# A two-layer hybrid block: the adaptive-norm background is placed elsewhere and fetched further ahead, and operand splits and weight sums of the feed-forward layers go from GpSimd to VectorE

## The chip, the cores and the metric

The kernel runs on one core of a Trainium2 chip, in one launch. The metric is the device time of an execution in microseconds (us). The core has five engines with a queue each, and a queue is worked off in order: TensorE (PE in the rows; its weight loads stand as PEld), VectorE (DVE), ScalarE (ACT), GpSimd (POOL) and SyncE (SP), which here only issues transfers.

## The reference

The input is x of 1024 tokens by 1024 features. There are two layers of two sub-blocks each. Every sub-block is wrapped in the same way:

```python
shift, scale, gate = split(silu(c) @ ada_w[layer, s] + ada_b[layer, s], 3)
h = rms_norm(x, norm_pre[layer, s]) * (1.0 + scale) + shift
y = sub_block(h)
x = x + gate * rms_norm(y, norm_post[layer, s])
```

Sub-block 0 of layer 0 is a mixer of two recurrent groups (gated delta rule and RWKV-7), sub-block 0 of layer 1 is a gated linear recurrence (RG-LRU), and sub-block 1 of both layers is a feed-forward layer of width 2816: `(silu(h @ w_gate) * (h @ w_up)) @ w_down`. All data is float32.

## The kernel before

The order of the program is: start and mixer, then three sub-blocks in `layers` (L893): n = 0, the feed-forward layer 0; n = 1, the recurrence; n = 2, the feed-forward layer 1. Tokens are worked in two halves of 512 columns, h = 0 and h = 1.

**Products.** A float32 operand is split into a high part (ScalarE casts it to fp32r) and a low part (the operand minus the high part, a subtraction of two tiles). A product of 512 features takes 12 matmuls: high by high, high by low and low by high, for 4 tiles of 128 rows. One pass of 512 columns is one matmul.

**Feed-forward** (`ffn`, L656). Gate and up projection of both halves are computed with seven products in place of eight, on sums and differences of the token operands (`operands`, L711) and of the weights (`sums`, L739). It has 22 steps f of 128 output columns. `first(f)` (L695) does two of the seven products, which need no sums; `second(f)` and `third(f)` do the other five. The first 10 or 14 `first` are run ahead of `operands`, the last four of them between its four parts. `rest` (L792) then runs second and third of every f, and in its later part the `first` that are still left. So a step is 5 products in the first twelve or so steps and 7 after.

**Who does what before.** `operands` makes five operands for each of four k: up to 6 additions on VectorE, five casts on ScalarE (L734) and five low parts (L735). Of the low parts, GpSimd takes those for which `out in (t3, b22)` holds: Python compares the lists by value, so for k = 0, where the lists are empty, that is four of five, and two of five for k = 1 to 3: ten in a layer. In every step `sums` has two additions on GpSimd (L744 and L746) and two on VectorE (L745, L747), and `third` lets GpSimd make the low part of one weight operand (`parts(a22, nc.gpsimd)`, L770). `first` makes two low parts on GpSimd.  VectorE also reads the results out of PSUM (L759, L761, L764, L774, L778) and multiplies them.

**Down projection** (`down`, L591). 22 (or 8) weight rows k for each of two column halves, in four PSUM banks. In the middle of the first column half it calls `aside`, which can start the next sub-block's norm.

**The background.** `ada_steps` (L500) computes one sub-block's shift, scale and gate on VectorE: six blocks of 512 columns (0 to 3 are shift and scale, 4 and 5 the gate), each of eight additions (L478, L480) of a 128x512 weight tile that a 256 KB transfer brings (L515). A block's sum is held in a tile of the ring `ad` (4 buffers), the weight tiles in three fixed tiles that are free after the mixer (`abufs`: g2, w2a2, k16; shown as g, w2a, k). A block ends with a small matmul into the one PSUM bank `es`, which `second` also uses. `operands` uses the ring `ad` too. A call of `tick` (L240) advances the background by one addition. Ticks stand in `down` (one for each k), in `rest` (one for each f) and in the recurrence's projections; `park` finishes a block, `drain` everything.

**What sets the order.** The code is written as one program; the framework's planner puts each engine's instructions in order before the run: at each point an instruction whose inputs and buffers are there may go, the earliest in the program first. So an addition of the background may be issued well before its place in the program. Once planned, an engine's queue is fixed, and an instruction that waits holds up all behind it on that engine. All transfers go through SyncE's queue.

Of the kernel before, what the change touches and what calls it, by code (L numbers as in the profile page):

```python
# [15 lines left out]
ALU = mybir.AluOpType  # L16
# [56 lines left out]
class Block:  # L73
# [426 lines left out]
    def ada_steps(self, l, s, tag, blocks, res, gtag):  # L500


        nc, a = self.nc, self.a
        w = a["ada_w"][l, s]
        if 0 in blocks:
            ab = self.c.tile([128, 24], F32, name=f"ab{l}{s}")
        res["G"] = []
        for cb in blocks:
            acc = self.t(tag, [128, 512])
            self.held = True  # L510
            for k in range(KD):
                st = next(self.abufs, None)
                if st is None:
                    st = self.t(tag, [128, 512])
                nc.sync.dma_start(st, w[k * 128:(k + 1) * 128, cb * 512:(cb + 1) * 512])  # L515
                self.ada_add(acc, st, k)
                yield
            if cb < 4:
                self.ada_put(ab, self.ada_total(acc), cb, l, s)
                if cb == 3:  # L520
                    res["A"], res["B"] = ab[:, 16:24], ab[:, 0:8]
            else:
                ps = self.t("es", [128, 512])
                o = (cb - 4) * 512
                br = self.t(tag, [128, 512])
                nc.sync.dma_start(br[0:1], a["ada_b"][l, s:s + 1, 2048 + o:2560 + o])
                nc.vector.tensor_tensor(acc[0:1], acc[0:1], br[0:1], ALU.add)
                self.mm(ps, self.ones, acc)
                wp = self.t(tag, [128, 512])
                nc.sync.dma_start(wp, a["norm_post"][l, s, o:o + 512].partition_broadcast(128))  # L530
                g = self.t(gtag, [128, 512])
                nc.vector.tensor_tensor(g, ps, wp, ALU.mult)
                res["G"].append(g)
            self.held = False
            yield
# [120 lines left out]
    def ffn(self, l, hs):  # L656
# [54 lines left out]
        def operands(xs):  # L711

            tags = iter(("p",) * 12 + ("s1",) * 8 + ("cy",) * 12 + ("s2",) * 4)
            A = E
            for k in range(4):
                v12 = self.modulated(self.turned_x(xs, k, ("sb", "es")), *self.AB, k, "ad")
                v22 = self.modulated(self.turned_x(xs, k + 4, ("sa",)), *self.AB, k + 4, "ad")
                (h1, l1), (h2, l2) = b11[k], b21[k]
                d1 = A()
                tt(d1, v12, f32(h1), ALU.subtract)  # L720
                tt(d1, d1, f32(l1), ALU.subtract)
                d2 = A()
                tt(d2, v22, d1, ALU.subtract)
                tt(v12, v22, v12, ALU.subtract)
                for full, out in ((d2, t2), (d1, t1), (v12, t3), (v22, b22), (None, t4)):
                    if full is None:
                        tt(d2, f32(h2), d2, ALU.subtract)
                        tt(d2, d2, f32(l2), ALU.add)
                        full = d2
                    if out is t4 and k > 1:  # L730
                        hi, lo = self.pair("ar")
                    else:
                        hi, lo = self.t(next(tags), [128, 512], F32R), self.t(next(tags), [128, 512], F32R)
                    nc.scalar.copy(hi, full)  # L734
                    (nc.gpsimd if out in (t3, b22) else nc.vector).tensor_tensor(lo, full, hi, ALU.subtract)  # L735
                    out.append((hi, lo))
                yield

        def sums(f):  # L739

            a11, a12 = fetch("ffn_w_gate", f)
            a21, a22 = fetch("ffn_w_up", f)
            s1, s2, s3, s4 = Y(), E(), E(), Y()
            nc.gpsimd.tensor_tensor(s1, a21, a22, ALU.add)  # L744
            tt(s2, s1, a11, ALU.subtract)  # L745
            nc.gpsimd.tensor_tensor(s3, a11, a21, ALU.subtract)  # L746
            tt(s4, a12, s2, ALU.subtract)  # L747
            return s1, s2, s3, s4, a22

# [17 lines left out]
        def third(f):  # L767

            s0, s4, a22, u2, u3, pc, pd = kept.pop(f)
            w3, w4 = parts(s4), parts(a22, nc.gpsimd)  # L770
            product(pd, w3, b22, False)
            following(f + 1)
            y = E()
            tt(y, pd, u2, ALU.add)  # L774
            self.act(y, y, AF.Silu)
            product(pc, w4, t4, False)
            tt(u3, u3, y, ALU.mult)
            tt(u2, pc, u2, ALU.add)  # L778
            tt(u2, u2, s0(), ALU.mult)  # L779
            for h, g in ((1, u3), (0, u2)):  # L780
                hi = self.t("yx", [128, 512], F32R)
                nc.scalar.copy(hi, g)  # L782
                tt(g, g, f32(hi), ALU.subtract)
                nc.sync.dma_start(self.gpart(h, f, 0), f32(hi))
                nc.sync.dma_start(self.gpart(h, f, 1), g)
# [3 lines left out]
                w = sums(f)  # L789
                kept[f, "w"] = w + (parts(w[1]),)  # L790

        def rest(ahead):  # L792
            following(0)
            for f in range(NF):
                second(f)
                if ahead <= f + 1 < NF:
                    first(f + 1)
                third(f)
                self.tick()

        return first, operands, rest

# [90 lines left out]
    def layers(self, hs, AB, x1, x2, x3, late):  # L893
# [3 lines left out]
        res = [dict() for _ in subs]  # L897
        for n, (l, x_in, x_out) in enumerate(subs):
            if n == 0:
                self.bg = chain(self.ada_steps(0, 1, "ad", (4, 5), res[0], "st"), self.ada_steps(1, 0, "ad", range(6), res[1], "gb"))  # L900
            else:
                self.bg = self.ada_steps(*ids[n + 1], "ad", range(6), res[n + 1], "st") if n + 1 < len(subs) else iter(())
            self.AB = AB
            gs = {}
            if l is not None:
                first, operands, rest = self.ffn(l, hs)
                if n == 0:
                    for f in range(PRE):
                        first(f, True)
                    xs = late()  # L910
                    self.deepen()
                ahead = (PRE if n == 0 else 0) + MID
                for f in range(ahead - MID, ahead - 4):
                    first(f, True)
                self.park()
                for f, _ in zip(range(ahead - 4, ahead), operands(xs)):
                    first(f, True)
                rest(ahead)
            for h in range(2):
                keep = h == 1 and l is None  # L920
                if l is None:
                    self.pool_lo = True
                    ys, w = self.lru(h, hs)
                    self.pool_lo = False
                    lhs = lambda k, half: ys[k]
                else:
                    w = self.a["ffn_w_down"][l]
                    for f in range(AHEAD if h == 0 else 0):
                        gs[0, f] = self.load_g(0, f)

                    def lhs(k, half):
                        if half == 0 and h == 0 and k + AHEAD < NF:
                            gs[0, k + AHEAD] = self.load_g(0, k + AHEAD)
                        g = gs[h, k]
                        if half == 1 and h == 0 and k >= 2:
                            gs[1, k - 2] = self.load_g(1, k - 2)
                        return g

                    if h == 1:
                        for f in (NF - 2, NF - 1):  # L940
                            gs[1, f] = self.load_g(1, f)
                nxt = []

                def aside():
                    if h == 0:
                        if l is None:
                            nxt.append(self.prenorm(x_in, 1, *AB))
                    elif n + 1 < len(subs):
                        self.drain()
                        nxt.append((res[n + 1]["A"], res[n + 1]["B"]))  # L950
                        nxt.append(self.prenorm(x_out, 0, *nxt[0]))

                last = n + 1 == len(subs) and h == 1
                xs = self.down(lhs, w, h, x_in, x_out, res[n]["G"], F_BANKS[4:] + F_BANKS[:4],
                               "s2" if keep else "yx", ("cy", 6) if keep else ("ht", 7) if last else (None, 0), keep, aside,
                               "lru" if l is None else None)
                if nxt:
                    hs = nxt[-1]
                    if h:
                        AB = nxt[0]  # L960
# [607 lines left out]
```

## Time and profile before

Times of three runs: 2782.76, 2784.68 and 2784.86 us; the median is 2784.68. The profiled execution took 2782.86 us, its span (first to last instruction) 2781.1 us.

| engine | busy us | share of the span |
|---|---|---|
| TensorE | 2639.1 | 95% |
| VectorE | 1779.6 | 64% |
| ScalarE | 1176.4 | 42% |
| GpSimd | 553.3 | 20% |

Shares are means over stages that differ. The stretches that the change touches are, in us from the span's start: operands of layer 0 from 1062 to 1109, its steps to about 1480, its down projection to 1720, the recurrence to about 2080, operands of layer 1 from 2116 to 2163, its steps to about 2525. "Granted clock" is the share of full speed that TensorE was given: 1.0 is 2.4 GHz, 0.5 is 1.2 GHz.

### The profile page before, as it was taken

Reading aid. Unit: us, or ns where it says so; the run is one execution under the profiler, and the core shown is the slowest. Engines: PE = TensorE matmul, PEld = TensorE weight load, DVE = VectorE, ACT = ScalarE, POOL = GpSimd, SP = SyncE. Lnnn points to the kernel's source line nnn. Section 1 sums busy time; section 2 is a strip of 40 time slices with the busy share of each in tenths; the row PEclk is TensorE's granted clock in tenths of the full one; section 3 lists DMA queues with packets and bytes.
Section 4 is the critical chain, followed back from the end, with each engine's and each line's share of the span. In section 5 each row is a group of like instructions: output and inputs, shape, how many; then the busy total and the mean of one; then the engine's idle time right before and its main releaser. Section 6 shows DMA issues by size and latency. Waiting matters only on the chain. (4 is left out here: it accounts for less than half of the span.)

```text
span 2781.1 us, 44135 instructions
## 1 busy us (share of the span) xinstructions
PE 2639.1 (95%) x16104; PEld 2041.2 (73%) x16104; DVE 1779.6 (64%) x3224; ACT 1176.4 (42%) x2164; POOL 553.3 (20%) x440
## 2 busy tenths in 40 slices
PE   7899999999999997899999999999998899999998
PEld 3666667676766676787888778777876788888887
DVE  5677878667677556988544463996855884553233
ACT  3555564553455435233332233572645333332222
POOL 2322220002100115233330000210015333330000
PEclk9999999999999999999999999999999999999999
DMA  6644443335732374766448873888754554448753
GB/s 237 226 150 136 139 151 101 118 108 202 250 110 81 99 243 148 237 209 196 150 137 300 291 247 130 293 296 298 257 196 148 166 191 139 137 142 288 239 180 108
DMA packets 423327, 519.60 MB, mean 187 GB/s; under 512 B 32667, under 2 KB 217790, under 8 KB 423110
## 3 DMA queue, kind: packets, MB, share of 16 engines
q1 hardware_dynamic: 423110, 516.78, 56.0%
q8 instruction: 127, 2.08, 0.3%
q14 instruction: 90, 0.74, 0.1%
HBM read 367.76 MB, written 148.90 MB: 186 GB/s over the span
## 5 line engine op out<-in xcount | busy, mean ns | idle before, releaser
L98 PE MATMUL mm<-ht,wh 128*128 128x512 f32 x1920 | 658.6, 417 | 27.4 <-ACT e L701 19.1
L98 PEld LDWEIGHTS mm<-ht,wh 128*128 128x128 f32 x1920 | 352.9, 192 | 117.1 <-ACT e L701 30.0
L98 PE MATMUL mm<-ht,wl 128*128 128x512 f32 x960 | 391.4, 409 | 9.6 <-DMA wl<-pd 4.4
L675 POOL TENSOR_TENSOR wl<-wd,wh 128x512 fp32r<-128x512 f32 x99 | 130.9, 1323 | 524.0 <-ACT wh L674 483.8
L98 PEld LDWEIGHTS mm<-ht,wl 128*128 128x128 f32 x960 | 183.8, 191 | 55.1 <-DMA wl<-pd 6.0
L144 ACT CAST wh<-wd 128x512 fp32r<-128x512 f32 x168 | 104.0, 620 | 263.1 <-PE sb L98 215.3
L145 DVE TENSOR_TENSOR wl<-wd,wh 128x512 fp32r<-128x512 f32 x156 | 108.1, 694 | 161.1 <-ACT wh L144 158.8
L145 POOL TENSOR_TENSOR wl<-wf,wh 128x512 fp32r<-128x512 f32 x80 | 115.6, 1453 | 290.1 <-ACT wh L144 232.0
L552 POOL TENSOR_TENSOR sm<-sm,dv 128x1 f32<-128x1 f32 x64 | 39.4, 625 | 651.9 <-DVE sm L551 338.9
L144 ACT CAST wh<-wf 128x512 fp32r<-128x512 f32 x133 | 82.0, 619 | 157.5 <-PE sb L98 78.4
L106 ACT ACTIVATE e<-mm 128x512 f32<-128x512 f32 x120 | 71.3, 594 | 146.0 <-PE mm L98 144.0
L675 DVE TENSOR_TENSOR wl<-e,wh 128x512 fp32r<-128x512 f32 x88 | 61.3, 696 | 105.1 <-ACT wh L674 105.1
L98 PE MATMUL sa<-s,wh 128*128 128x512 f32 x392 | 121.2, 391 | 0.0
L674 ACT CAST wh<-wd 128x512 fp32r<-128x512 f32 x99 | 61.3, 621 | 131.0 <-PE sb L98 43.2
L106 ACT ACTIVATE e<-e 128x512 f32<-128x512 f32 x140 | 88.0, 631 | 57.4 <-DVE e L774 24.6
L106 ACT ACT_TABLE_LOAD x84 | 107.8, 1283 | 2.2 <-PEq L1557 0.7
L674 ACT CAST wh<-yx 128x512 fp32r<-128x512 f32 x88 | 54.6, 621 | 125.3 <-PE sb L98 48.4
L98 PEld LDWEIGHTS <-h 64*64 64x64 f16 (+1 forms) x1984 | 53.8, 106 | 73.4 <-issue 49.2
L1198 POOL TENSOR_TENSOR s<-s,k 128x512 f32<-128x512 f32 x16 | 24.7, 1543 | 340.0 <-DVE s L1441 163.5
L98 PE MATMUL sa<-wh,p 128*128 128x512 f32 x260 | 91.8, 397 | 0.0
L782 ACT CAST yx<-yx 128x512 fp32r<-128x512 f32 x88 | 54.6, 621 | 77.3 <-DVE yx L779 40.5
L98 PEld LDWEIGHTS sa<-s,wh 128*128 128x128 f32 x392 | 73.7, 188 | 15.5 <-issue 0.4
(494 smaller groups left out, 6633.5 us busy)
## 6 DMA issues: line engine op xcount, KB each, us to landing
gd<-yx SPq DMA_DIRECT2D x176, 256.0 KB
pd<-wh SPq DMA_DIRECT2D x132, 256.0 KB
pd<-wl SPq DMA_DIRECT2D x132, 256.0 KB
wd<-in_ffn_w_down_dram SPq DMA_DIRECT2D x132, 256.0 KB
wh<-pd SPq DMA_DIRECT2D x120, 256.0 KB
wl<-pd SPq DMA_DIRECT2D x120, 256.0 KB
wd<-in_ffn_w_gate_dram SPq DMA_DIRECT2D x114, 256.0 KB
wd<-in_ffn_w_up_dram SPq DMA_DIRECT2D x78, 256.0 KB
```

Of the source, the lines that this page charges most:

```text
L98: self.nc.tensor.matmul(out, lhsT=lhsT, rhs=rhs, start=start, stop=stop, skip_group_check=more)
L106: return self.nc.scalar.activation(out, in_, func, bias=bias, scale=scale)
L144: nc.scalar.copy(wh, wf)
L145: (nc.gpsimd if self.pool_lo and (self.pool_lo > 1 or k0) else nc.vector).tensor_tensor(wl, wf, wh, ALU.subtract)
L552: nc.gpsimd.tensor_tensor(r, r, self.mhalf[:, 0:1], ALU.pow)
L674: nc.scalar.copy(flat(wh), full)
L675: (eng or nc.vector).tensor_tensor(flat(wl), full, flat(wh), ALU.subtract)
L782: nc.scalar.copy(hi, g)
L1198: nc.gpsimd.tensor_tensor(im, first, one32, ALU.add)
```

## The change

Four things are changed. (1) In `operands` all low parts go to VectorE; in `sums` both GpSimd additions go to VectorE; in `third` the low part of a22 goes to VectorE. `first` stays as it is. (2) `ada_steps` issues the transfers of up to three weight tiles before the addition that uses the first of them. (3) `rest` ticks only from f = 12 on in layer 0 (from f = 0 in layer 1). (4) The background of layer 1's feed-forward layer is cut in two: its blocks 0 to 3 are appended to the background of n = 0 and go on through n = 1, and its gate blocks 4 and 5 are ticked in n = 2, where nothing was ticked before. `aside` no longer drains the background but ticks until what the next norm needs is in the program.

```diff
@@ ada_steps
-        res["G"] = []
+        res.setdefault("G", [])
...
+            sts = []
             for k in range(KD):
-                st = next(self.abufs, None)
-                if st is None:
-                    st = self.t(tag, [128, 512])
-                nc.sync.dma_start(st, w[k * 128:(k + 1) * 128, cb * 512:(cb + 1) * 512])
-                self.ada_add(acc, st, k)
+                for j in range(len(sts), min(k + 3, KD)):
+                    st = next(self.abufs, None)
+                    if st is None:
+                        st = self.t(tag, [128, 512])
+                    nc.sync.dma_start(st, w[j * 128:(j + 1) * 128, cb * 512:(cb + 1) * 512])
+                    sts.append(st)
+                self.ada_add(acc, sts[k], k)
@@ operands
-                    (nc.gpsimd if out in (t3, b22) else nc.vector).tensor_tensor(lo, full, hi, ALU.subtract)
+                    tt(lo, full, hi, ALU.subtract)
@@ sums
-            nc.gpsimd.tensor_tensor(s1, a21, a22, ALU.add)
+            tt(s1, a21, a22, ALU.add)
             tt(s2, s1, a11, ALU.subtract)
-            nc.gpsimd.tensor_tensor(s3, a11, a21, ALU.subtract)
+            tt(s3, a11, a21, ALU.subtract)
@@ third
-            w3, w4 = parts(s4), parts(a22, nc.gpsimd)
+            w3, w4 = parts(s4), parts(a22)
@@ rest
-        def rest(ahead):
+        def rest(ahead, late):
...
-                self.tick()
+                if f >= late:
+                    self.tick()
@@ layers
-                self.bg = chain(self.ada_steps(0, 1, "ad", (4, 5), res[0], "st"), self.ada_steps(1, 0, "ad", range(6), res[1], "gb"))
-            else:
-                self.bg = self.ada_steps(*ids[n + 1], "ad", range(6), res[n + 1], "st") if n + 1 < len(subs) else iter(())
+                self.bg = chain(self.ada_steps(0, 1, "ad", (4, 5), res[0], "st"), self.ada_steps(1, 0, "ad", range(6), res[1], "gb"),
+                                self.ada_steps(1, 1, "ad", range(4), res[2], None))
+            elif n == 2:
+                self.bg = self.ada_steps(1, 1, "ad", (4, 5), res[2], "st")
...
-                rest(ahead)
+                rest(ahead, 12 if n == 0 else 0)
...
-                        self.drain()
+                        while "A" not in res[n + 1] or n == 0 and len(res[1]["G"]) < 2:
+                            self.tick()
```

## Rows read from the trace of the kernel before

**Rows 1.** The page, engines: busy us (share of the span) x instructions.

```profile
PE 2639.1 (95%) x16104; PEld 2041.2 (73%) x16104; DVE 1779.6 (64%) x3224; ACT 1176.4 (42%) x2164; POOL 553.3 (20%) x440
```

**Rows 2.** Stretches: us, busy us (x instructions) by engine, granted clock, DMA share, GB/s.

```profile
1066.00:1112.00 46.00, 31.81 (x128) 24.79 (x128) 39.82 (x40) 24.60 (x44) 28.23 (x18) 0.85 0.41 130
...
1112.00:1190.00 78.00, 68.54 (x284) 54.34 (x283) 71.31 (x97) 21.53 (x36) 24.11 (x16) 0.96 0.73 237
...
1190.00:1250.00 60.00, 60.00 (x270) 49.73 (x270) 52.15 (x69) 21.61 (x36) 17.69 (x12) 1.00 0.62 205
...
1300.00:1480.00 180.00, 180.00 (x792) 147.09 (x791) 96.96 (x148) 65.54 (x111) 54.52 (x43) 1.00 0.50 161
...
2117.00:2162.00 45.00, 31.75 (x130) 24.48 (x128) 38.51 (x35) 24.25 (x43) 29.70 (x20) 0.86 0.34 111
...
2170.00:2290.00 120.00, 120.00 (x531) 99.39 (x530) 104.64 (x133) 42.63 (x71) 39.72 (x26) 1.00 0.59 193
```

**Rows 3.** TensorE's waits, 1056 to 1112: us in total, times, longest.

```profile
PE mm L98 <- ACT e L701: 6.8, 2, 3.7
PE es L98 <- ACT wh L674: 6.3, 1, 6.3
PE mm L98 <- POOL wl L675: 1.0, 1, 1.0
```

**Rows 4.** TensorE's waits, 2112 to 2170.

```profile
PE es L98 <- ACT wh L674: 7.0, 1, 7.0
PE mm L98 <- ACT e L701: 6.7, 2, 3.7
```

**Rows 5.** TensorE's waits, 1112 to 1270.

```profile
PE sb L98 <- DVE yx L761: 5.7, 3, 3.3
PE sa L98 <- DVE yx L764: 5.7, 3, 2.6
```

**Rows 6.** Stretches at half clock, columns as in rows 2.

```profile
1152.50:1159.30 6.80, 5.64 (x13) 4.46 (x14) 6.53 (x10) 1.11 (x2) 1.82 (x1) 0.50 0.76 223
1261.70:1265.10 3.40, 3.40 (x10) 2.62 (x9) 3.37 (x6) 0.63 (x1) 0.00 (x0) 0.50 0.90 278
...
2159.40:2166.20 6.80, 3.72 (x9) 2.95 (x10) 5.42 (x7) 2.28 (x4) 1.77 (x2) 0.50 0.40 116
```

**Rows 7.** VectorE in order of time: start, us, what [idle before <- releaser].

```profile
2118.38 0.68 DVE L724 TENSOR_TENSOR ad<-ad,ad 128x512 f32<-128x512 f32 x1
2118.98 0.69 DVE L723 TENSOR_TENSOR e<-ad,e 128x512 f32<-128x512 f32 x1
2125.00 1.77 DVE L727 TENSOR_TENSOR e<-ht,e 128x512 f32<-128x512 f32 x1 [5.33 <-POOL p L735]
2126.80 1.66 DVE L728 TENSOR_TENSOR e<-e,ht 128x512 f32<-128x512 f32 x1
```

**Rows 8.** GpSimd in the same stretch, in order of time.

```profile
2124.92 1.29 POOL L735 TENSOR_TENSOR p<-e,p 128x512 fp32r<-128x512 f32 x1
2126.18 1.73 POOL L735 TENSOR_TENSOR p<-ad,p 128x512 fp32r<-128x512 f32 x1
```

**Rows 9.** VectorE's waits, 1056 to 1112.

```profile
DVE cy L735 <- ACT cy L734: 0.7, 1, 0.7
```

**Rows 10.** The chain that ended last: start, us, what.

```profile
2172.68 2.72 PE sb L98 x12
```

**Rows 11.** VectorE's groups, 1112 to 1190: busy, mean ns | idle before.

```profile
L480 DVE SCALAR_TENSOR_TENSOR ad<-w2a,sc,ad 128x512 f32<-128x512 f32 x9 | 10.3, 1147 | 2.0 <-DMA w2a<-in_ada_w_dram 1.9
L480 DVE SCALAR_TENSOR_TENSOR ad<-k,sc,ad 128x512 f32<-128x512 f32 x9 | 8.8, 979 | 1.5 <-DMA k<-in_ada_w_dram 1.3
L480 DVE SCALAR_TENSOR_TENSOR ad<-g,sc,ad 128x512 f32<-128x512 f32 x8 | 7.0, 873 | 0.0
...
L761 DVE TENSOR_TENSOR yx<-sb,yx 128x512 f32<-128x512 f32 x5 | 3.4, 682 | 0.1
```

**Rows 12.** A group of GpSimd, 1112 to 1190, columns as in rows 11.

```profile
L744 POOL TENSOR_TENSOR yx<-wd,wd 128x512 f32<-128x512 f32 x6 | 9.8, 1629 | 10.6 <-DMA wd<-in_ffn_w_up_dram 8.1 <-DVE ad L480 2.5
```

**Rows 13.** TensorE's waits, 1590 to 2060.

```profile
PE sa L98 <- DVE wl L145: 8.7, 9, 1.9
PE mm L98 <- DMA wl<-pd: 4.4, 2, 3.5
```

## The prediction

> **What bounds the kernel now.** I read the page first: TensorE is busy 95% of the span [rows 1], so a gain can only come from stretches in which it stands still or runs at half clock. The table of stretches finds them. In the operands of both feed-forward layers TensorE is busy 31.8 of 46 us and 31.75 of 45 us, and in the first steps of layer 0 68.5 of 78; in the steps after that, and in those of layer 1, it is busy throughout (60.0 of 60, 120.0 of 120) [rows 2]. VectorE is the fullest other engine exactly there. The waits then name what TensorE stood for: in the operands of layer 0 14.1 us for ScalarE's casts and copies and one low part (6.8 + 6.3 + 1.0) [rows 3], in those of layer 1 13.7 us [rows 4], in the steps of layer 0 11.4 us for VectorE's reads out of PSUM (L761, L764) [rows 5]. The timeline shows why VectorE is late. Alone it starts a two-tile subtraction every 0.60 us (2118.38, 2118.98); while GpSimd works, the same operation takes 1.66 to 1.77 us (2125.00, 2126.80) [rows 7], and GpSimd's own goes from 1.29 to 1.73 [rows 8]. Reads out of PSUM stay at 0.68 in a stretch full of GpSimd work (the last of [rows 11]). So a GpSimd subtraction of two tiles takes about 1.07 us from VectorE (1.67 less 0.60), more than the 0.60 that VectorE would need to do it. Last, the chain: from 2165 to the end it is nearly all TensorE, 2.72 us per product of 12 matmuls [rows 10]; a microsecond saved ahead of it moves the end.
>
> **Operands.** Between 2117 and 2162 VectorE ran 35 instructions in 38.5 us [rows 2]. At 0.605 each that is 21.2, so 17.3 us is what GpSimd cost it. GpSimd ran 20 there: by the code ten low parts of `operands`, three weight sums, six low parts of `first`, one small one. Thirteen move. VectorE then has 48 instructions, 29.0 us; of the six low parts that stay two fall into VectorE's pause of 5.33 us and four still cost 1.07 each, 4.3. The sum is 33.3, which is 5.2 less. The pause ended with a GpSimd low part [rows 7], which waited its turn behind other GpSimd work; on VectorE it can follow its cast, and I take 1 us of the pause. New is that ten low parts wait for a cast on ScalarE, and VectorE's next additions queue behind them, and TensorE behind those through ScalarE; the one such wait shown is 0.7 us [rows 9]. I give that 0.2: 6 us gained in layer 1. In layer 0 VectorE ran 40 instructions in 39.8 us [rows 2]; 52 by 0.605 plus 4.3 is 35.8, so 4 gained and 1 of the pause: 5 us. Ends: 7.9 us lost per layer if no slow instruction gets faster (13 by 0.605), and all of 14.1 and 13.7 gained. TensorE also loses after each stop. At half clock 9 matmuls took 3.72 us [rows 6]; at the full rate (2.72 us for 12) they take 2.04. I take 1 us back per layer. Operands: 6 + 5 + 2 = 13 us.
>
> **Steps.** A step of five products is 13.6 us of TensorE [rows 10]. Counted in the code, VectorE has 15 large instructions in it and GpSimd three; afterwards VectorE has 18, which is 10.9 us at 0.605. From 1190 to 1250, 4.4 steps without background, VectorE was busy 52.15 us with 69 instructions [rows 2], 0.756 each; afterwards 69 + 13 by 0.605 is 49.6. So it is no fuller than before, and TensorE did not wait there, nor in the steps of layer 1 with the same load. The stops come where the background is added: 26 large additions ran between 1112 and 1190, with means of 0.87 to 1.15 us for 0.75 [rows 11]. Under six ticks belong to these steps, so the planner had drawn them forward into what it held for VectorE's free time, and GpSimd made that time not free. Afterwards the free time is 2.7 us a step, room for three additions, and the instructions keep to it. The stretch loses 11.4 us in waits [rows 5] and, at half clock, 13 matmuls in 5.64 us and 10 in 3.40 [rows 6], for 2.95 and 2.27 at full rate: 3.8 more. Of these 15.2 us I take 11. What is late next is the weight transfer: GpSimd waited 8.1 us for the up-projection's tiles before L744 [rows 12]; the same instruction on VectorE would hold up the reads out of PSUM behind it, and so TensorE. I take 2 of these into the 4.2 us that stay. Ends: 0 to 15.2 gained, or a loss as in the rival below.
>
> The Trainium skill, "Perfetto Trace Analysis", section "Optimizing Scalar/DVE Operations", says that with a saturated VectorE it may make sense to offload to ScalarE or even GpSimd, though the shared read port may undo that. By its first half the change makes the bound engine fuller, which is the rival below; rows 7 bear out the second half. The Trainium skill, "SBUF — State Buffer", section "Who interferes with whom", has the loser blocked for the whole of the other's instruction: 1.29 rather than 1.07 us for each of the four that stay, or 0.9 us more per layer.
>
> **Late ticks, prefetch, queue.** With ticks from f = 12 the additions lose their place in the program, but they never ran at their place; what holds them back is the ring of four sums. I cost the later place at nothing: VectorE's free time hides it, and without it each addition is 0.75 us. The transfers keep their number and size in SyncE's queue; the three tiles were refilled as they fell free, so the fetch ahead mostly changes rank. In the steps 3.2 us of waits for these tiles are at stake [rows 11], inside the 4.2. In down projection and recurrence TensorE waits 8.7 us for low parts on VectorE [rows 13], some of them behind an addition that waits for its tile, and 4.4 us for stored weights; taking 16 additions and 4 MB out of the recurrence can only help these, the new order may not. I take 1, with ends of 8.7 either way. For the mixer, where the fetch ahead is the only edit, I take 0, and up to 4 either way, about half of that.
>
> **Gate blocks in layer 1.** 16 additions, 12 us, join steps in which VectorE has room (104.6 of 120 before, about 80% afterwards): 0. If they are drawn forward they hold up to three of the four `ad` buffers during the operands: up to 9 us lost (four parts, each 2.2 longer, three additions of 0.75).
>
> **Sum.** 13 + 11 + 1 = 25 us off 2782.86 is 2757.9 for a profiled execution; the runs' median is 1.8 above it. Predicted: 2760, own range 2748 to 2770.
>
> **Rivals.** (a) *VectorE becomes the bound of the step.* With 18 instructions at full length (0.69) a step is 12.4 us, three additions make it 14.6, against 13.6 of TensorE: 1.0 by 12 steps, 12 us in layer 0, and the transfer waits of 8.1 come in line, 20 in all, and the 15.2 of before stay. Less 13 in the operands this is 7 slower, and about as much as 5 more if layer 1 with its 16 additions follows: 2795. It decides from the point at which VectorE's step passes 13.6. For it: 87% busy before. Against: 0.60 apart, not 0.69 [rows 7], and TensorE at 120 of 120 [rows 2]. (b) *Half the gain.* The planner refills VectorE to the brim, or the gate blocks hold the `ad` buffers: the 11 of the steps stay lost, or 9 of the operands: 2771. For it: additions run wherever there is room. (c) *The placement matters.* The additions leave the operands and the first twelve steps: the 15.2 are gained, 3 more in the operands (four additions) and 4 of the 8.7: 35 us, 2750 or a little lower. Against: no addition kept to its place before. (d) *The change doesn't reach TensorE*: other waits end as late, 2784.
>
> **How the numbers follow.** Forecast 0.55, (a) 0.12, (b) 0.17, (c) 0.11, (d) 0.05. The range 2742 to 2786 leaves most of (a) and the tail of (c) out. What differs by less than 0.2% (5.6 us) can't be told from no change. Faster: forecast, (b) and (c) less a little, 0.80; same: (d) and the edge of (b), 0.08; slower: (a), 0.12.
>
> **What would show it.** GpSimd's instructions fall from 440 to 288 (152: 10 low parts and 66 others per layer). In both operand stretches instructions of 1.7 us on VectorE fall from some 15 to four or five, and the longest stop of TensorE from 6.3 and 7.0 us to under 3. In the first steps of layer 0 TensorE's waits for L761 and L764 fall below 4 us, and the half clock there goes. VectorE in the steps stays under 90%. Wrong it would be if VectorE's slow instructions stay, if TensorE waits for L744's sum or for VectorE in layer 1's steps, or if the operands of layer 1 wait for `ad`.

## The result, and the profile after

The changed kernel takes 2744.24 us (median of four runs, 2738.0 to 2750.65) against 2783.8 for the kernel before in the same comparison: a ratio of 0.9857, 95% interval 0.9837 to 0.9877, or 39.6 us less. The forecast was 2760, a gain of 25. The profiled execution, 2738.0 us with a span of 2736.2, is the fastest of the four, so of the 44.9 us between the two spans some 5 are its own luck.

Where they went, by stage. Each stage goes from one marker instruction to the next; the times are differences of starts in the profiled executions. The markers, in lines of the kernel before, are the first L1330 in the mixer, the first L701, L720 (operands), L759 of steps 0, 12 and 21, and the same again in layer 1. So "recurrence and down 0" holds the down projection of layer 0 and the recurrence. The last two rows are experiments told below: the change in two halves.

| us | start | mixer | recurrence and down 0 | operands 0 | first 12 steps 0 | operands 1 | first 12 steps 1 |
|---|---|---|---|---|---|---|---|
| before | 158.2 | 761.4 | 652.5 | 49.9 | 182.1 | 50.9 | 179.8 |
| after | 151.8 | 755.7 | 644.1 | 44.7 | 165.3 | 44.9 | 180.7 |
| engine moves only | 157.5 | 761.6 | 652.1 | 45.3 | 166.7 | 43.4 | 179.6 |
| background only | 156.9 | 754.4 | 644.8 | 50.9 | 174.9 | 50.9 | 187.0 |

The stages not shown differ by at most 2 us between before and after. So 11.2 us come from the operands, 16.8 from layer 0's first steps, 8.4 from down projection and recurrence, 5.7 from the mixer and 6.4 from the start; the other stages, layer 1's first steps among them, give 3.6 back.

The page after, engines, answers to [rows 1]. GpSimd has 152 instructions fewer, VectorE 152 more, and VectorE's busy time rose by only 34.4 us for them, 0.23 each:

```profile
PE 2618.2 (96%) x16104; PEld 2030.5 (74%) x16104; DVE 1814.0 (66%) x3376; ACT 1178.8 (43%) x2164; POOL 336.9 (12%) x288
```

Stretches after, columns as in [rows 2]: operands of layer 0, first twelve steps of layer 0, the steps behind them, operands and first steps of layer 1.

```profile
1056.00:1098.00 42.00, 32.29 (x135) 25.29 (x134) 36.11 (x53) 24.82 (x44) 8.05 (x6) 0.88 0.46 146
...
1098.00:1264.00 166.00, 164.19 (x721) 134.55 (x720) 150.90 (x243) 56.99 (x96) 0.00 (x0) 1.00 0.72 232
1264.00:1433.00 169.00, 169.00 (x744) 138.14 (x743) 113.96 (x166) 61.60 (x105) 20.69 (x16) 1.00 0.45 143
...
2077.00:2122.00 45.00, 35.29 (x148) 27.69 (x147) 39.15 (x56) 26.02 (x47) 8.53 (x7) 0.89 0.50 158
2122.00:2302.00 180.00, 180.00 (x791) 147.82 (x790) 147.09 (x229) 64.43 (x108) 7.76 (x6) 1.00 0.58 187
```

In the first steps of layer 0 GpSimd does nothing any more; VectorE runs 243 instructions in 150.9 us, 0.62 each, and TensorE is busy 164.19 of 166 us at the full clock.

TensorE's waits after, in the operands of layer 0 (1045 to 1110) and in its first steps (1098 to 1270); they answer to [rows 3] and [rows 5]:

```profile
PE es L98 <- ACT wh L677: 5.2, 1, 5.2
PE mm L98 <- ACT e L704: 4.3, 2, 2.6
PE mm L98 <- POOL wl L678: 0.2, 1, 0.2
...
PE sb L98 <- DVE yx L764: 1.6, 2, 1.4
```

The waits of 11.4 us for reads out of PSUM are down to 1.6; those of the operands, 14.1, to 9.7. In layer 1 the rows are the same (5.2, 4.3, 0.2), 9.7 for 13.7 [rows 4].

What a meeting costs now. VectorE and GpSimd in layer 1's operands after, in order of time (start, us, what):

```profile
2088.68 0.68 DVE L738 TENSOR_TENSOR p<-ad,p 128x512 fp32r<-128x512 f32 x1
2089.28 1.77 DVE L723 TENSOR_TENSOR e<-ad,ht 128x512 f32<-128x512 f32 x1
2090.97 0.68 DVE L738 TENSOR_TENSOR p<-e,p 128x512 fp32r<-128x512 f32 x1
2091.58 0.68 DVE L724 TENSOR_TENSOR e<-e,ht 128x512 f32<-128x512 f32 x1
```

```profile
2089.19 1.31 POOL L678 TENSOR_TENSOR wl<-wd,wh 128x512 fp32r<-128x512 f32 x1 [0.99 <-ACT wh L677]
```

VectorE starts an instruction each 0.60 us; the one that meets GpSimd's subtraction takes until 2090.97, 1.69 us, so 1.09 more than its due, as in [rows 7]. VectorE instructions of more than 1 us fell in the operands from 15 and 16 to 4 in each layer, in layer 0's first steps from 29 to none.

### The profile page after: what moved, and what is told of

Read it like the earlier page. It is cut to its first block, busy times and chain, and to the rows that moved or that the text cites. A ratio compares the mean times of both kernels' runs of the same rounds, so it can differ in the third digit from the quotient of the medians.

```text
span 2736.2 us, 44054 instructions
## 1 busy us (share of the span) xinstructions
PE 2618.2 (96%) x16104; PEld 2030.5 (74%) x16104; DVE 1814.0 (66%) x3376; ACT 1178.8 (43%) x2164; POOL 336.9 (12%) x288
## 5 line engine op out<-in xcount | busy, mean ns | idle before, releaser
L98 PE MATMUL mm<-ht,wl 128*128 128x512 f32 x960 | 389.9, 408 | 11.4 <-DMA wl<-pd 5.9
L678 POOL TENSOR_TENSOR wl<-wd,wh 128x512 fp32r<-128x512 f32 x60 | 78.0, 1299 | 580.0 <-ACT wh L677 379.5
L98 PEld LDWEIGHTS <-h 64*64 64x64 f16 (+1 forms) x1984 | 53.4, 106 | 71.8 <-issue 47.6
L677 ACT CAST wh<-e 128x512 fp32r<-128x512 f32 x88 | 54.5, 619 | 98.9 <-PE sa L98 43.7
L678 DVE TENSOR_TENSOR wl<-e,wh 128x512 fp32r<-128x512 f32 x88 | 60.5, 687 | 44.2 <-ACT wh L677 44.2
L145 DVE TENSOR_TENSOR wl<-wf,wh 128x512 fp32r<-128x512 f32 x53 | 36.5, 690 | 69.2 <-ACT wh L144 67.2
```

Of the source, the lines that this page charges most:

```text
L98: self.nc.tensor.matmul(out, lhsT=lhsT, rhs=rhs, start=start, stop=stop, skip_group_check=more)
L145: (nc.gpsimd if self.pool_lo and (self.pool_lo > 1 or k0) else nc.vector).tensor_tensor(wl, wf, wh, ALU.subtract)
L677: nc.scalar.copy(flat(wh), full)
L678: (eng or nc.vector).tensor_tensor(flat(wl), full, flat(wh), ALU.subtract)
```

## The experiments

Each was timed beside the kernel before, whose median was 2783.97, 2785.05 or 2784.31 us, and gains are against the median beside it. Theory 1: a two-tile operation on GpSimd costs VectorE more than VectorE needs to do it, and this contention is where the feed-forward layers lost. Rival: what matters is where the background stands and how early its tiles come.

**Engine moves only.** The kernel before with part (1) of the change and nothing else:

```diff
-                    (nc.gpsimd if out in (t3, b22) else nc.vector).tensor_tensor(lo, full, hi, ALU.subtract)
+                    tt(lo, full, hi, ALU.subtract)
...
-            nc.gpsimd.tensor_tensor(s1, a21, a22, ALU.add)
+            tt(s1, a21, a22, ALU.add)
...
-            w3, w4 = parts(s4), parts(a22, nc.gpsimd)
+            w3, w4 = parts(s4), parts(a22)
```

(the second sum likewise).

> The kernel before with the engine moves alone (low parts of the operands, weight sums and low part of a22 on VectorE); fetch and place of the background as before. Theory 1 (GpSimd's two-tile work slows VectorE; the moves carry the gain of both operand stretches and of the first steps of layer 0): about 28 us less than before, 2750 to 2762; operands shorter by 5 and 6 us, the first 12 steps of layer 0 by 14 to 17. Theory 2 (the steps of layer 0 got shorter because the additions of the background have other places): operands shorter by 11 together, steps as before, about 2773.

Measured: 2754.94 us, ratio 0.9905 [0.9886, 0.9925], 29.0 less. The gain stands where theory 1 puts it: operands 49.9 to 45.3 and 50.9 to 43.4, first steps of layer 0 182.1 to 166.7, and no other stage changes by more than 0.7 us.

**Background only.** The changed kernel with part (1) undone (the diff above, reversed).

> The changed kernel with the engine moves undone: fetch ahead, late ticks and the split background alone. Theory 1: operands and steps as long as before, a gain only in mixer, down projection and recurrence, about 12 us in all: 2764 to 2776. Theory 2: the first 12 steps of layer 0 are shorter by 14 to 17 us too: about 2756.

Measured: 2771.85, ratio 0.9963 [0.9949, 0.9978], 12.1 less. With the 29.0 this makes 41.1 for the two halves, 39.6 for the whole: they add up, within the intervals. The time is in theory 1's range, but by luck in part: that theory wanted operands and steps as long as before, and the table shows a sum of unlike signs: mixer 7.0 and down projection and recurrence 7.7 gained, first steps of layer 0 7.2 gained (25 additions of L480 fall there in place of 32), and 7.2 lost in those of layer 1, where the gate blocks now run beside GpSimd's work. VectorE's groups in those steps of layer 1 (2149 to 2336) show the meetings by their mean, 1398 and 919 ns for 744 undisturbed, and TensorE's waits there (second fence) what came of it; in the changed kernel it has none of either:

```profile
L480 DVE SCALAR_TENSOR_TENSOR ad<-w2a,sc,ad 128x512 f32<-128x512 f32 x3 | 4.2, 1398 | 0.1
L480 DVE SCALAR_TENSOR_TENSOR ad<-k,sc,ad 128x512 f32<-128x512 f32 x4 | 3.7, 919 | 1.0 <-DMA k<-in_ada_w_dram 1.0
L480 DVE SCALAR_TENSOR_TENSOR ad<-g,sc,ad 128x512 f32<-128x512 f32 x4 | 3.0, 744 | 0.0
```

```profile
PE sb L98 <- DVE yx L764: 2.1, 1, 2.1
PE sa L98 <- DVE yx L767: 1.4, 1, 1.4
```

**Unread work on GpSimd.** The changed kernel, with a subtraction on GpSimd beside each of the 152 moved operations; its result goes to a tile that nobody reads:

```diff
+        def idle_work(x):
+            nc.gpsimd.tensor_tensor(self.t("jk", [128, 512], BF16), f32(x), f32(x), ALU.subtract)
...
                     tt(lo, full, hi, ALU.subtract)
+                    if out in (t3, b22):
+                        idle_work(hi)
...
+            if more:
+                idle_work(flat(wh))
```

(`more` is set for the parts of s1, s3 and a22.)

> The changed kernel, and beside every moved instruction GpSimd again does a subtraction of two tiles whose result nobody reads (10 a layer in the operands, 3 in each step); VectorE depends on none of it. Theory 1 (shared access to the tiles): VectorE's instructions of 1.7 us come back, the operands are 6 to 10 us longer in each layer and the first steps of layer 0 longer by 10 or more: 2764 to 2780. Rival (before, VectorE and ScalarE were late because they waited for GpSimd's results): as the changed kernel, 2740 to 2750.

Measured: 2771.82, ratio 0.9961 [0.9949, 0.9973]. Against the changed kernel 27.6 us come back, though nothing reads these results: the slow instructions on VectorE come from contention and not from the order of the results. By stages the operands are 8.7 and 7.8 us longer than in the changed kernel (53.4 and 52.7), as expected, the first steps of layer 0 8.2 (173.5), less than the 10 expected, and those of layer 1 4.1 (184.8). One thing is not clean: in each operand stretch the trace names an unread subtraction as the last thing that a cast on ScalarE waited for (3.4 and 2.7 us; releasers are inferred). In layer 0's first steps ScalarE waits for nothing of GpSimd's. The stretches, operands of layer 0 and of layer 1:

```profile
1060.00:1112.00 52.00, 36.97 (x141) 28.57 (x140) 47.80 (x55) 25.09 (x44) 27.03 (x18) 0.80 0.40 125
2110.00:2160.00 50.00, 34.67 (x132) 26.71 (x131) 49.65 (x59) 22.04 (x39) 24.36 (x17) 0.83 0.40 126
```

VectorE takes 0.87 us for each instruction (47.80 by 55) where the changed kernel has 0.68 (36.11 by 53), and TensorE's granted clock is 0.80 for 0.88.

**The two groups of moves apart.** The kernel before with the first hunk of that diff (the low parts of operands), and the kernel before with the others (the steps' sums and low part).

> The kernel before with one edit only: the ten low parts of operands per layer are computed on VectorE. Theory (a two-tile subtraction on GpSimd takes 1.07 us from VectorE, more than the 0.60 it takes there): each operand stretch is 4 to 6 us shorter, the steps stay as before, 10 to 12 us gained in all. Rival, the additions drawn into the steps depend on how the operands end: then the steps of layer 0 change by more than 3 us as well.

> The kernel before with the other edit only: the two weight sums and one low part of each step are computed on VectorE. Theory: the first twelve steps of layer 0 gain 14 to 16 us, their instructions of 1.7 us on VectorE go, the operands gain 1 to 2 (three sums of the first steps fall there), 15 to 18 us in all, which with the edit of the operands makes the 29 of both. Rival, contention from the low parts of operands reaches into the steps through the additions drawn forward: less than 10.

Measured: 2772.7, ratio 0.9958 [0.9942, 0.9973], 11.6 less; and 2766.95, ratio 0.9937 [0.9917, 0.9956], 17.4 less. The sum is 29.0, that of both together. The first takes the operands to 43.8 and 44.6 and leaves layer 0's first steps at 179.7 (before 182.1); the second leaves layer 0's operands at 49.5 (before 49.9) and takes the steps to 168.0.

**Fetch ahead alone, and everything but it.**

```diff
             for k in range(KD):
-                st = next(self.abufs, None)
...
+                for j in range(len(sts), min(k + 3, KD)):
+                    st = next(self.abufs, None)
```

> The kernel before with the fetch ahead alone. In the changed kernel the mixer, where nothing else was edited, was about 6 us shorter between its first chunk and its end, and 6 us before that. If the fetch ahead does that: 2772 to 2778, with fewer waits of VectorE for the background's tiles. Rival (the order is only another one, and the start's clock differs from run to run): within 3 us of before.

> The changed kernel with the transfer of each weight tile issued at its own addition again. If the fetch ahead brings the mixer's 5 to 6 us: about 2750, with the loss before 760 us and nearly nothing after it. Rival (the gain there came with any new order of the program): 2741 to 2748.

Measured: alone 2779.32, ratio 0.9981 [0.9968, 0.9993], 4.7 less; without it 2747.24, ratio 0.9871 [0.9853, 0.9889], 3.0 above the changed kernel. By the medians neither theory came in: fetch alone lies just outside the 2772 to 2778, and the kernel without it inside its rival's 2741 to 2748. The profiles are plainer. The mixer took 751.0 to 759.7 us in the nine profiled kernels with fetch ahead and 760.9 to 762.2 in the five without. In fetch alone a part is given back behind it (operands of layer 0 49.9 to 51.1, its first steps 182.1 to 183.3, down projection and recurrence 652.5 to 654.3). The mixer's stretch in which it gains, before (first fence) and in fetch alone (second):

```profile
640.00:680.00 40.00, 36.31 (x238) 26.01 (x235) 29.43 (x61) 14.72 (x32) 6.27 (x5) 0.91 0.63 209
680.00:725.00 45.00, 40.30 (x220) 30.63 (x219) 29.90 (x56) 12.32 (x29) 17.91 (x14) 0.96 0.73 255
```

```profile
640.00:680.00 40.00, 38.04 (x209) 27.94 (x210) 32.57 (x59) 15.09 (x32) 9.25 (x6) 0.96 0.82 270
680.00:725.00 45.00, 40.54 (x345) 30.62 (x344) 31.34 (x62) 11.77 (x25) 14.20 (x13) 1.00 0.81 273
```

The transfers move 270 GB/s for 209, 16 background additions run between 560 and 725 for 7 before, and TensorE is granted 0.96 and 1.00 of its clock for 0.91 and 0.96. Over the whole mixer TensorE's waits are 22.6 us before and 21.3 after; its busy time falls from 737.7 to 734.0 for the same products, and its mean granted clock rises from 0.99 to 1.00, so most of the 5.7 goes with the clock. That the fetch ahead shortens the mixer is shown; why TensorE runs at the full clock for more of it was not isolated.

**Ticks from f = 0 in layer 0.**

```diff
-                rest(ahead, 12 if n == 0 else 0)
+                rest(ahead, 0)
```

> The changed kernel with ticks from the first step on in layer 0 (f = 0 instead of 12). If the planner draws the additions forward in any case (as the prediction costed it): within 3 us of the changed kernel, 2741 to 2748. If the late ticks are what spares the first steps: 5 to 8 us slower, with the first 12 steps of layer 0 that much longer; in the run with the background edits alone these steps were 7 us shorter than before.

Measured: 2751.56, ratio 0.9881 [0.9866, 0.9896], 7.3 above the changed kernel and so outside the 3 us expected, though the intervals overlap. The other case has the time (5 to 8 slower) but not the place, as it wanted the first steps that much longer: they take 166.6 us for 165.3, with 31 additions in them for 24. Down projection and recurrence take 647.3 for 644.1, at a granted clock of 0.98 for 0.99; 3.8 more are in the start, which the edit doesn't touch. So the late ticks do keep seven additions out of the steps, and bring little there. The profiled execution (2746.77) is the fastest of its four: what the others lose, no trace shows, and what the late ticks are worth in all stays open.

**What holds the operands now.** After the change TensorE still stands 9.7 us in each operand stretch, 5.2 of it in one stop. Three edits of the changed kernel move work around that stop: the four operand parts two `first` earlier, two more `first` behind the operands, and the sums and parts of step 0's weights before the last part:

```diff
-                for f in range(ahead - MID, ahead - 4):
+                for f in range(ahead - MID, ahead - 6):
...
-                for f, _ in zip(range(ahead - 4, ahead), operands(xs)):
+                for f, _ in zip(range(ahead - 6, ahead - 2), operands(xs)):
                     first(f, True)
+                for f in range(ahead - 2, ahead):
+                    first(f, True)
```

```diff
-AHEAD, PRE, MID = 6, 4, 10
+AHEAD, PRE, MID = 6, 4, 12
```

(with the edit above). The third takes `following(0)` out of `rest`:

```diff
                 for f, _ in zip(range(ahead - 4, ahead), operands(xs)):
                     first(f, True)
+                    if f == ahead - 2:
+                        following(0)
```

> The changed kernel with the four parts of the operands put two first() earlier, so that two of them come after the operands. If TensorE's 9.5 us of stops in each operand stretch are left because VectorE is the bound and nothing else is ready: the stops shrink by 5 to 9 us in each layer, 10 to 16 us in all with the half clock, about 2730. Rival (ScalarE's queue ties those first() to VectorE's casts, so that they stop as well): within 4 us of the changed kernel.

> The changed kernel with two more first() run ahead in each layer, both after the operands (16 and 12 in place of 14 and 10), which costs 512 KB of stores and 512 KB of loads for each. If it is the amount of other work for TensorE that counts: as early_operands, about 2730. If it is the start of the operands that counts: between the changed kernel and early_operands, 2735 to 2744.

> The changed kernel with the sums and parts of step 0's weights issued before the last of the four operand parts instead of after it. In the changed kernel the longest stop of TensorE in each operand stretch (5.2 us) ends with the cast of those weights, which stand behind the last part on VectorE (eleven instructions from 1085.0 to 1091.7) and on ScalarE. Theory, it is this order: the es product then begins as soon as the last part's first operand is cast, the stop of 5.2 falls below 2 in both layers, and the five instructions moved ahead delay the last part by 3 us, which its products hide for the most part; TensorE's idle time in the operands falls from 9.5 to 5 to 7, and the time by 4 to 8 us. Rival, VectorE's whole work of the stretch sets its length (busy 36.1 of 42 us): the stop only moves to another place, and the time stays within 2 us of the changed kernel's.

Measured: 2741.36, ratio 0.9849 [0.9834, 0.9864]; 2743.44, ratio 0.9864 [0.9845, 0.9882]; 2744.33, ratio 0.9855 [0.9834, 0.9875]. None can be told from the changed kernel, so the theories that wanted 2730, or 4 to 8 us, missed, and the time stayed where the rivals had it. In the last the stop of 5.2 fell to 2.6, and the others grew; with two more `first` it fell to 1.4, and a wait of 2.7 for ScalarE's activation came in its place. TensorE's waits in layer 0's operands, with two more `first`:

```profile
PE mm L98 <- ACT e L704: 4.0, 3, 2.0
PE mm L98 <- ACT e L106: 2.7, 1, 2.7
PE es L98 <- ACT wh L677: 1.4, 1, 1.4
PE mm L98 <- POOL wl L678: 1.0, 1, 1.0
```

9.1 us in all for 9.7 (8.7 in the last run): the order mostly shifts the stops. What is left is the amount of work on VectorE, and the next run takes from that.

**All low parts on VectorE.** The changed kernel, and the two low parts of `first` leave GpSimd too:

```diff
-            product(pa, parts(a11, nc.gpsimd), b11, True)
+            product(pa, parts(a11), b11, True)
...
-            product(pa, parts(a12, nc.gpsimd), b21, False)
+            product(pa, parts(a12), b21, False)
```

> The changed kernel with the last GpSimd work of the feed-forward layers, the two low parts of first, on VectorE too. By the price of 1.07 us against 0.60 each of the six that fall into an operand stretch saves VectorE 0.47 us: 2 to 3 us gained per layer at the most, and nothing in the steps, where TensorE no longer waits (VectorE goes from about 60% to below 70% after step 12): 2 to 5 us faster than the changed kernel. Rival, the low parts now stand in VectorE's order behind their cast and hold up what follows: 2 to 10 us slower.

Measured: 2736.81, ratio 0.9828 [0.9806, 0.985], the lowest median of all, 7.4 under the changed kernel; the intervals overlap, so the two are not told apart by time alone. The trace shows the part that is the edit's: operands of 41.2 and 40.8 us for 44.7 and 44.9, more than the 2 to 3 expected of each, no instruction over 1 us left on VectorE there, and TensorE's waits in layer 0's operands 6.0 for 9.7:

```profile
PE es L98 <- ACT wh L677: 2.9, 1, 2.9
PE mm L98 <- DVE wl L678: 1.4, 2, 1.0
PE mm L98 <- ACT e L106: 1.0, 1, 1.0
PE mm L98 <- ACT e L704: 0.7, 1, 0.7
```

The wait that the rival named, for low parts that are now in VectorE's order, is there (L678, 1.4), and smaller than what is saved.

## Why the prediction was right, and where not

**What bounds the kernel: right for the moves.** TensorE's stops in three stretches, and a price of 1.07 us for each meeting on VectorE. The unread work shows that the price is contention: 152 subtractions brought 27.6 us back, and the moves alone had taken 29.0 away. What the change gained besides came from stages that the prediction had not counted among those three. The Trainium skill, "SBUF — State Buffer", section "Who interferes with whom", has the second of the two blocked until the first has finished. The prediction read that as the whole of 1.29 us; counted from VectorE's issue, the GpSimd operation shown above had 1.22 left (2090.50 less 2089.28), and VectorE lost 1.09, so the trace agrees to 0.13 us in this meeting. The Trainium skill, "Perfetto Trace Analysis", section "Optimizing Scalar/DVE Operations", lets a saturated VectorE offload to GpSimd, with the doubt that it might not help; the moves back, 29.0 us faster, decide for the doubt.

**Operands: right.** Forecast 6 + 5 + 2 = 13; the stretches lost 6.0 and 5.2, and the run with this edit alone 11.6. The forecast of four slow instructions left per layer holds (4 and 4). (Of the 20 GpSimd operations counted in layer 1 the last was no small one but a seventh low part of `first`; it changes nothing here.) One sign failed: the longest stop was to fall below 3 and is 5.2. The sum had not asked for that sign: 14.1 less 5 and 13.7 less 6 leave 9.1 and 7.7 us of stops, and 9.7 were left in each layer. VectorE's pause, from which the working took 1 us, was 5.3 us in both layers before ([rows 7], and the first line here, of layer 0, 1056 to 1112) and is 3.7 in both after (second line, 1045 to 1110); it ends with ScalarE's cast now, 1.6 sooner:

```profile
DVE e L727 <- POOL p L735: 5.3, 1, 5.3
...
DVE p L738 <- ACT p L737: 3.7, 1, 3.7
```

No other wait of VectorE's for a cast of the operands is left. The stop at the end is the length of the last part's chain on VectorE: from 1085.01 to 1093.47 VectorE starts an instruction every 0.52 to 0.67 us without a pause, three of them additions of the background. So another order mostly moves the idle time elsewhere, and less work on VectorE shortens it (the experiments on it).

**Steps: right in kind, too small.** Forecast 11 of the 15.2 at stake. The moves alone gained 15.4 in this stretch, the whole, and the changed kernel 16.8. The term that was mis-sized is the 4.2 kept back, 2 of them for weight transfers: the 8.1 us that GpSimd waited for the up-projection's tiles [rows 12] did not come over to VectorE. Its groups after, 1098 to 1264:

```profile
L747 DVE TENSOR_TENSOR yx<-wd,wd 128x512 f32<-128x512 f32 x12 | 8.2, 687 | 0.0
...
L480 DVE SCALAR_TENSOR_TENSOR ad<-g,sc,ad 128x512 f32<-128x512 f32 x8 | 6.0, 751 | 0.1
L480 DVE SCALAR_TENSOR_TENSOR ad<-k,sc,ad 128x512 f32<-128x512 f32 x8 | 6.0, 750 | 0.0
L480 DVE SCALAR_TENSOR_TENSOR ad<-w2a,sc,ad 128x512 f32<-128x512 f32 x8 | 6.0, 749 | 0.0
```

Idle before the sum of L747: nothing. GpSimd had reached it early and waited; on VectorE it comes in its turn, when the tile has landed. The additions run at 0.75 and are 24, for 32 before; the moves alone had 31 of them there and took 166.7 us, so their number matters little once nothing meets them. VectorE is at 91% there, above the 90% given as a sign, which failed, and it does no harm: 12.5 us by step (150.9 us of 166, for 12 steps of 13.8) against TensorE's 13.6. Rival (a) would have decided above that, and fell.

**Late ticks, prefetch, queue: the step that failed.** It was costed at 1 us, 0 for the mixer and 1 for down projection and recurrence, and these gave 5.7 and 8.4. For the ticks themselves 0 is near what the trace shows (1.3 us in the steps), but by the median of that run it is open; and the ring alone does not hold the additions back, as seven of 31 left the steps with the later ticks. The mixer's share comes from the fetch ahead, and lies just outside the 4 us given either way: "mostly changes rank" overlooked that the rank is the point, as 16 additions for 7 get done in that stretch. Down projection and recurrence gained what the 8.7 in the ends allowed. It is the placement: these stages took 644 to 648 us with it (after 644.1, background only 644.8, no fetch ahead 648.0) and 651 to 654 without (before 652.5, moves only 652.1, the two groups of moves 654.0 and 651.0, fetch alone 654.3). VectorE's additions there, before (1464 to 2117) and after (1433 to 2077):

```profile
L480 DVE SCALAR_TENSOR_TENSOR ad<-g,sc,ad 128x512 f32<-128x512 f32 x17 | 12.8, 750 | 11.2 <-DMA g<-in_ada_w_dram 11.1
L480 DVE SCALAR_TENSOR_TENSOR ad<-k,sc,ad 128x512 f32<-128x512 f32 x16 | 12.0, 750 | 14.7 <-DMA k<-in_ada_w_dram 14.5
L480 DVE SCALAR_TENSOR_TENSOR ad<-w2a,sc,ad 128x512 f32<-128x512 f32 x16 | 12.0, 749 | 8.8 <-DMA w2a<-in_ada_w_dram 8.6
```

```profile
L480 DVE SCALAR_TENSOR_TENSOR ad<-k,sc,ad 128x512 f32<-128x512 f32 x14 | 10.5, 749 | 2.7 <-DMA k<-in_ada_w_dram 2.7
L480 DVE SCALAR_TENSOR_TENSOR ad<-w2a,sc,ad 128x512 f32<-128x512 f32 x14 | 10.5, 749 | 4.6 <-DMA w2a<-in_ada_w_dram 4.4
L480 DVE SCALAR_TENSOR_TENSOR ad<-g,sc,ad 128x512 f32<-128x512 f32 x13 | 9.8, 750 | 4.0 <-DMA g<-in_ada_w_dram 3.9
```

The waits of VectorE for a background tile, with all that is queued behind it, fell from 34.7 us (11.2, 14.7 and 8.8) to 11.3. Fetch alone leaves them at 36.0, the change without it has 13.0: not the earlier fetch but the placement did that. It leaves fewer additions there (41 for 49), but their number alone does not set the wait: with ticks from f = 0 there are 35, and they wait 18.0. The prediction had the rows of TensorE's low-part waits [rows 13] and not these. TensorE's waits in the stretch of [rows 13], after (1557 to 2022):

```profile
PE sa L98 <- DVE wl L145: 6.1, 4, 2.3
PE mm L98 <- DMA wl<-pd: 5.9, 2, 5.0
```

The low parts give 2.6 of the 8.4, the stored weights take 1.5 back. Over the two stages all of TensorE's waits fell from 29.4 to 25.1 us, and its granted clock was 0.99 in both. So 4.3 of the 8.4 are waits, and 4.0 are less busy time (623.0 to 619.0) for the same products. Why that fell, and how the waits on VectorE and on TensorE hang together, is open.

**Gate blocks in layer 1: right, for one more reason than given.** Forecast 0; the first steps of layer 1 lost 0.9. With GpSimd's work still in them (background only) they lost 7.2. That they cost so little depends on the moves. Four of the additions were drawn forward into layer 1's operands, which take 44.9 us with them and 43.4 with the moves alone; no instruction there waits for an `ad` buffer.

**The start: not forecast, and its cause open.** The 6.4 us of the profiled execution lie ahead of all that was edited but the fetch ahead. Fourteen profiled kernels have starts of 150.3 to 161.8 us; with fetch ahead they were 150.3 to 157.8, without 157.5 to 161.8. In the stretch from 20 to 35 us, where TensorE is busy 14.64 us in both kernels, it was granted 0.82 before and 1.00 after. How much of the start is chance and how much the fetch ahead is open.

**The sum.** Forecast 25, measured 39.6 by medians: operands 11.6 of 13, steps 17.4 of 11 with their edit alone, and the background 12.1 for 1. So 2744.24 lies below the forecast case's own range of 2748 to 2770, and is held only by the outer one, from 2742. It is nearest to the 2750 of rival (c), but not by its way: (c) had the additions leave the operands and the first twelve steps, and 4 and 24 of them still run there, for 3 and 32 before. The moves did what the forecast says of them, and more in the steps; the placement mattered behind the steps, and the fetch ahead in the mixer.

## What to carry to other kernels

Before giving VectorE's work to GpSimd, or taking it back, measure a meeting: VectorE's spacing with and without a GpSimd operation beside it. Where the difference is larger than VectorE's own time for the operation, and something waits for VectorE, it belongs on VectorE even if that is the fuller engine. Where nothing waits it is all the same: in layer 1's first steps 20 VectorE instructions of over 1 us became 4 with the moves alone, and the stretch took 179.6 us for 179.8. Background work that waits for its transfers is not free because an engine has room: read the idle time before each of its groups, as an in-order queue passes that wait on to what stands behind it.

## What had not been expected of the hardware

Work on GpSimd that nobody reads cost 27.6 us: 152 operations, most of them of 1.23 us, 0.18 us of the end for each. The price is paid where VectorE is short of time, in the operands and first steps of both layers, and was nothing in layer 0's steps after the twelfth (169.1 us with the unread work and 43 GpSimd operations, 169.6 in the changed kernel with 16).

The changed kernel's executions spread over 12.7 us (2738.0 to 2750.65) where before spread over 2.1 beside it; over all its executions the kernel before had 2772.95 to 2793.94. One profiled execution can be off by as much as a term of the sum, so stage times were compared over several kernels.
